# Small tiles padded to 64 bytes in a one-core decoder layer, and three small copies moved from VectorE to ScalarE

## The chip, the cores and the metric

One Trainium2 chip, one of its cores. The metric is device time in microseconds of one launch: the median of three runs of the kernel before is 544.61 us (544.2 to 545.45).

## What is computed

One layer of a decoder trunk over 256 tokens of width 1024, in float32. Cut to what matters here:

```
h = rms_norm(x, norm_mix_g)
u, q, kc, vc, ks, vs, kw, vw, gates, g_conv, g_attn = split(h @ w_in)
conv = silu(layer_norm(depthwise_conv31(u_a * sigmoid(u_g)))) @ conv_pw_w
k_cmp, v_cmp = compress(kc, ...), compress(vc, ...)      # 15 blocks of 32 tokens
    # compress: z = einsum(blocks + pos, w1); silu(z) @ w2
attn = gated sum of compressed, selected and window attention (16 heads, 4 groups)
x = x + (sigmoid(g_conv) * conv + sigmoid(g_attn) * attn) @ w_out
x = x + cross_attention(rms_norm(x), mem)                # 4 heads of 256
x = x + swiglu(rms_norm(x))                              # 1024 -> 2 x 2816 -> 1024
out = rms_norm(x)
```

## The kernel before

Nearly all of the time is matrix products with 1024 x 256 weight blocks. They run on TensorE in `float32r`, a type that goes through the array in one pass, and the accuracy of float32 is put together from three such products: each operand is split into a high part (ScalarE, a copy that rounds, L174 and L287) and a low part (the difference, VectorE L176 and L288, or GpSimd for a range of weights), and `hi*hi + hi*lo + lo*hi` is summed in PSUM. One `nc.tensor.matmul` has a stationary operand (`lhsT`, loaded into the array, shown as LDWEIGHTS, engine PEld) and a moving operand (`rhs`, streamed through it, shown as MATMUL, engine PE).

The stages in order of time: keys of the cross-attention (`ps_k`), the convolution's input (`ps_u`), the attention's projections (`ps_kc` to `ps_vw`), the gates mixed with the attention's scores and outputs (`ps_ga`, `ps_gc`, `ps_v`, and `s`, `pt`, `o`), the convolution's and the mixer's output projections (`ps_pw`, `ps_wo`), the cross-attention (`ps_xq`, `xs`, `xo_ps`, `ps_xo`), the feed-forward input (`ps_f`, L1200 with 512 moving columns and L1202 with 256), and its output (`fo`, `m`, L1239, mostly 512 columns). In all projections written as `rows` (L243) without `nat`, the weights are stationary and the activations moving; in `vs`, `vw` and `v0` to `v3` it is the other way round.

All tiles in SBUF come from one pool `sb`, through two helpers: `long` (activations and other tiles of 8 KB a partition, L121) and `small` (all others, L133). A tag names a place that tiles share one after the other. The pool lays the places out one behind the other in each partition, in the order in which the program first asks for them, and rounds each up to a multiple of 32 bytes. In the built program:

- `ppt`, `cpt`, `ones`, `eps_t` lie at bytes 1,152, 3,264, 4,032 and 4,544 of the partition. `eps_t` has two numbers and takes 32 bytes.
- So the fourteen places of the long tiles lie from 4,576 on, each at a multiple of 64 plus 32.
- `roots0`, one number at 127,456, takes 32 bytes as well. All larger places behind it begin at a multiple of 64 again: the high and low halves of weights from 127,488 on, the raw weights, the scores, the transposed probabilities.

Counted over the 3,819 matmul instructions of the built program, by the place in a 64-byte line at which the moving and the stationary operand begin:

| moving, stationary begin at (of 64) | instructions | which |
|---|---|---|
| 32, 0 | 2,834 | projections of L243 with stationary weights (2,064), L1200 (352), L1202 (352), cross scores `xs` (48), L607 (16), L331 (2) |
| 0, 32 | 631 | `vs`, `vw`, `v` of L243 (288), L1239 (207), L692 (32), L789 (24), L795 and L798 (64), L1080 (16) |
| 32, 32 | 201 | `xo_ps` of L967 (48), scores L732 and L734 (64), L1239 (48), L273 (16), L468 and L474 (9), L521 (16) |
| 0, 0 | 134 | transposes L777, L879 and L1004 (116), warm-up and small sums (18) |
| others | 19 | L521 (16, moving at 36), L709 (2), L341 (1) |

Of the 256-column `float32r` products, 2,480 are of the first kind, 335 of the second and 80 of the third; of the 512-column ones 352 (L1200), 183 (L1239) and 80 (L732 and L1239).

Three small copies touch the compression of keys and values. For `kc` and `vc` (the loop at L498) the four groups are copied from PSUM on ScalarE; a fifth column of the tile, `GROUPS`, is set to zero on VectorE (L505), and two entries of it are filled with the position code, a copy of 16 numbers a partition from `ppt` (L506). In `hidden` (L514), the values' hidden layer is written to `zz` four times over (L534), 240 numbers on 64 partitions. All three are `nc.vector.tensor_copy`. The scheduler of the framework places each instruction on its engine's queue by priority and by what it depends on, and an engine runs its queue in order. `convolve` (L441) puts the taps of the depthwise convolution behind everything else on VectorE, ScalarE and GpSimd, as filler; `behind` lets it start after the marks that it is given, one of which is the copy of L506.

Of the kernel before, what the change touches and what calls it, by code (L numbers as in the profile page):

```python
# [11 lines left out]
AF = mybir.ActivationFunctionType  # L12
# [3 lines left out]
P = 128  # L16
# [4 lines left out]
GROUPS = 4  # L21
HD = 64
# [7 lines left out]
BIG = 1e30  # L30
NCMP = 15
WARM = 8
FIRST_G = 18

CHUNKS = (
# [12 lines left out]
PP_POS = PP_DW + NB * TAPS  # L48
# [48 lines left out]
def tile_hybrid_block(  # L97
# [16 lines left out]
    nc = tc.nc  # L114
    PSUM = bass.MemoryType.PSUM
    sb = ctx.enter_context(tc.tile_pool(name="sb", bufs=1))
# [14 lines left out]
        return t, t[:, 0], t[:, 1]  # L131

    def small(name, shape, dt=F32, tag=None, bufs=1):  # L133
        return sb.tile(shape, dt, tag=tag or name, name=name, bufs=bufs)

    def bank(name):
# [8 lines left out]
    def aux(name, shape, tag, bufs):  # L145
        return axp.tile(shape, F32, tag=tag, name=name, bufs=bufs)

    def f(ap):
        return ap.bitcast(F32)


    ppt = small("ppt", [P, PP_END])
# [13 lines left out]
    def col(base, j):  # L166
        return ppt[:, base + j:base + j + 1]
# [15 lines left out]
    def behind(*marks):  # L183

        stack = ExitStack()
        for m in marks:
            stack.enter_context(tc.issue_after(m.ins))
        return stack
# [40 lines left out]
    def in_line():  # L229
        return behind(*last)  # L230
# [23 lines left out]
    def gemm(name, x, nat=False):  # L254

        ps = bank(f"ps_{name}")
        for i in range(2):
            sweep(ps, halved(name, i), x, i, nat, name in in_order)
        return ps
# [86 lines left out]
    warm = aux("warm", [P, P], "o", 1)  # L346
    for _ in range(WARM):
        nc.tensor.matmul(warm, lhsT=ones, rhs=ones, start=True, stop=True)
# [35 lines left out]
    for i in range(4):  # L384
        hs = slice(2 * i, 2 * i + 2)
        for kb in (2 * i, 2 * i + 1):
            vec = nc.vector.scalar_tensor_tensor(out=hf[:, kb], in0=xt_t[:, kb], scalar=col(PP_GMIX, kb),
                                                 in1=r1, op0=ALU.mult, op1=ALU.mult)
# [14 lines left out]
    zz = small("zz", [P, 2, 4 * 64], tag="pr", bufs=4)  # L403
# [33 lines left out]
    taps = range(TAPS)  # L437
    on_v = chain(taps_v(0, taps[FIRST_G:], part01), *[taps_v(j, taps, yt[:, j:j + 2]) for j in range(2, NB, 2)])
    on_g = taps_g(taps[:FIRST_G])

# [10 lines left out]
    for j in range(NB):  # L451
# [3 lines left out]
        vec = nc.vector.tensor_tensor(out=vt[j][:, PAD:], in0=ps[:, 0], in1=sg, op=ALU.mult)  # L455
# [42 lines left out]
    for kv, name in enumerate(("kc", "vc")):  # L498
        ps = gemm(name, h)
        kc = kvt[kv]  # L500
        for g in range(2):
            for odd in range(2):
                at = ps[HD * g:HD * g + HD].rearrange("p b (m l o) -> p b l m o", l=8, o=2)[:, :, :, :, odd]
                act = nc.scalar.activation(kc[HD * odd:HD * odd + HD, :, g:GROUPS:2].rearrange("p l b m -> p b l m"), at, AF.Copy)
        nc.vector.memset(kc[:, :, GROUPS], 0.0)  # L505
        vec = nc.vector.tensor_copy(kc[:, :, GROUPS, 0:2],  # L506
                                    ppt[:, PP_POS + 16 * kv:PP_POS + 16 * kv + 16].rearrange("p (m l) -> p l m", m=2))
        convolve(14, 1 - kv, act, vec)
    kcp = small("kcp", [P, GROUPS, 2, 16], F32R)
    vcs = small("vcs", [P, 2, 2, HD], F32R, tag="sg", bufs=3)  # L510
# [3 lines left out]
    def hidden():  # L514


        z_ps = aux("z_ps", [P, GROUPS + 1, NCMP], "o", 1)
        with in_line():
            for l in range(16):
                for kv in range(2):  # L520
                    mm = nc.tensor.matmul(z_ps[HD * kv:HD * kv + HD], lhsT=w1t[:, kv, l],  # L521
                                          rhs=kvt[kv][:, l % 8, :, l // 8:l // 8 + NCMP], start=l == 0, stop=l == 15)
        last[:] = [mm]
        zs = small("zs", [P, GROUPS, NCMP], tag="zs", bufs=2)
        at = small("at", [P, 1])
        nc.scalar.activation(at, z_ps[:, GROUPS, 0:1], AF.Copy)
        sig = nc.scalar.activation(zs, z_ps[:, :GROUPS], AF.Sigmoid, bias=at)

        with behind(sig):
            nc.scalar.activation(small("exps", [P, 1]), eps1, AF.Exp)  # L530
        z1 = zz[:HD, 0, :64].rearrange("p (g n) -> p g n", g=GROUPS)[:, :, 0:NCMP]
        nc.vector.scalar_tensor_tensor(out=z1, in0=z_ps[:HD, :GROUPS], scalar=at[:HD], in1=zs[:HD], op0=ALU.add, op1=ALU.mult)
        nc.vector.scalar_tensor_tensor(out=zs[HD:], in0=z_ps[HD:, :GROUPS], scalar=at[HD:], in1=zs[HD:], op0=ALU.add, op1=ALU.mult)
        nc.vector.tensor_copy(zz[HD:, 1].rearrange("p (g r n) -> p g r n", g=GROUPS, r=4)[:, :, :, 0:NCMP],  # L534
                              zs[HD:].unsqueeze(2).to_broadcast([HD, GROUPS, 4, NCMP]))

    def compressed():

# [15 lines left out]
    for j in range(4):  # L554
# [6 lines left out]
        vec = nc.vector.scalar_tensor_tensor(out=q1[0:64], in0=ps[64:128], scalar=-0.125, in1=f(q1[64:128]),  # L561
                                             op0=ALU.mult, op1=ALU.subtract)
# [269 lines left out]
    p = [scores(0)]  # L832
# [6 lines left out]
    vec = nc.vector.tensor_tensor(out=nsc, in0=nsc, in1=mc.unsqueeze(3).to_broadcast([P, 2, HEADS, 16]), op=ALU.subtract)  # L839
# [10 lines left out]
    vec = nc.vector.tensor_tensor(out=nsc, in0=nsc, in1=sumc.unsqueeze(3).to_broadcast([P, 2, HEADS, 16]), op=ALU.mult)  # L850
# [632 lines left out]
```

## Time and profile before

| | us |
|---|---|
| median of three runs | 544.61 |
| the profiled execution's own time | 544.99 |
| span of its trace | 542.9 |
| busy: TensorE (PE), weight loads (PEld) | 535.8, 502.0 |
| busy: VectorE, ScalarE, GpSimd | 455.8, 358.1, 155.5 |

An engine's row in the profile gives its busy time, its share of the span and its instructions. A matmul's record runs from its issue to the modelled end of its pipeline, so the records of a stream overlap; the pace of the stream is the distance between starts. The view that shows this best is the chain that ended last: a row of it holds a start, a length, and a count of matmuls that followed each other without a gap, so that length by count is the pace. The timeline shows starts and the records of each group, and behind them the idle time before it and what ended it.

### The profile page before, as it was taken

The page shows a single profiled execution, that of the slowest core. Times are in us where ns is not written, and L with a number is a line of the kernel's source. Part 1 is how long each engine was busy: PE and PEld are TensorE (multiplying, and loading weights), DVE is VectorE, ACT ScalarE, POOL GpSimd, SP SyncE. Part 2 cuts the span into 40 slices and gives each one's busy share as a digit, 9 for nine tenths or more (in the row PEclk, how much of TensorE's full clock was granted, in tenths as well). Part 3 has the DMA queues.
Part 4 walks back from the last instruction along what each step waited for, and adds up shares of the span by engine and source line. Part 5 has one row for each costly group of instructions (what it writes and reads, how often), then busy time and mean ns, then how long its engine had stood idle before and what let it go on. Part 6 is the DMA issues. An engine that isn't in the chain of part 4 may idle for free.

```text
span 542.9 us, 10515 instructions
## 1 busy us (share of the span) xinstructions
PE 535.8 (99%) x3963; PEld 502.0 (92%) x3963; DVE 455.8 (84%) x916; ACT 358.1 (66%) x646; POOL 155.5 (29%) x109
## 2 busy tenths in 40 slices
PE   9999999999999999999999999999999999999995
PEld 8999999999999998999999999988888888888884
DVE  4898999899889898975859676688899998879996
ACT  4676566678855977879447655566666677638563
POOL 0079999998990000300004000240000000000001
PEclk9999999999999999999999999999999999999999
DMA  8927955554424653347655642847756668438632
GB/s 317 403 86 243 366 170 180 201 184 156 154 99 150 203 173 112 123 137 214 222 190 165 240 155 89 233 145 219 246 168 202 195 209 234 146 122 235 195 121 78
DMA packets 30740, 101.52 MB, mean 187 GB/s; under 512 B 3297, under 2 KB 5857, under 8 KB 30305
## 3 DMA queue, kind: packets, MB, share of 16 engines
q1 hardware_dynamic: 29104, 96.99, 53.5%
q0 software_dynamic: 864, 2.62, 2.9%
q10 hardware_dynamic: 720, 1.23, 0.6%
q8 instruction: 31, 0.51, 0.4%
q14 instruction: 21, 0.16, 0.1%
HBM read 99.59 MB, written 1.25 MB: 186 GB/s over the span
## 4 chain that ended last, share of the span: by engine, by line
PE 61%; DVE 1%; ACT 0%; issue 0%; DVEq 0%; ACTq 0%
PE ps_f L1200 15%; PE ps_f L1202 8%; PE fo L1239 6%; PE ps_pw L243 4%; PE ps_xq L243 4%; PE ps_wo L243 4%; PE ps_xo L243 4%; PE ps_v L243 4%; PE m L1239 4%; PE xo_ps L967 1%; PE xs L967 1%; PE o L798 1%; PE pt_a L777 1%; PE s L732 1%; PE o L795 1%; PE pt_b L777 0%
## 5 line engine op out<-in xcount | busy, mean ns | idle before, releaser
L419 DVE SCALAR_TENSOR_TENSOR yp<-vt,ppt,yp 128x256 f32<-128x256 f32 x196 | 78.5, 483 | 0.3
L1200 PE MATMUL ps_f<-g,f_1h 128*128 128x512 f32 x176 | 49.0, 397 | 0.0
L1200 PE MATMUL ps_f<-g,f_0h 128*128 128x512 f32 x176 | 48.2, 395 | 0.0
L1200 PEld LDWEIGHTS ps_f<-g,f_1h 128*128 128x128 f32 x176 | 32.8, 188 | 7.6 <-ACT f_1h L174 0.2
L1200 PEld LDWEIGHTS ps_f<-g,f_0h 128*128 128x128 f32 x176 | 30.0, 188 | 4.0
L176 DVE TENSOR_TENSOR f_1l<-f,f_1h 128x1024 fp32r<-128x1024 f32 x22 | 27.4, 1248 | 5.9 <-ACT f_1h L174 4.9
L1202 PEld LDWEIGHTS ps_f<-g,f_0l 128*128 128x128 f32 x176 | 27.0, 189 | 3.9
L174 ACT ACTIVATE f_1h<-f 128x1024 fp32r<-128x1024 f32 x22 | 23.2, 1056 | 7.7 <-PE ps_xo L243 3.7
L1202 PE MATMUL ps_f<-g,f_0l 128*128 128x256 f32 x176 | 28.3, 282 | 0.0
L176 DVE TENSOR_TENSOR f_0l<-f,f_0h 128x1024 fp32r<-128x1024 f32 x22 | 26.8, 1219 | 1.7 <-ACT f_0h L174 1.7
L1202 PE MATMUL ps_f<-g,f_1l 128*128 128x256 f32 x176 | 26.5, 281 | 0.0
L176 POOL TENSOR_TENSOR u_0l<-u,u_0h 128x1024 fp32r<-128x1024 f32 x7 | 17.3, 2467 | 31.4 <-DVE kt L505 30.5
L1203 ACT ACTIVATE ab<-ps_f 128x256 f32<-128x256 f32 x44 | 16.5, 374 | 12.4 <-PE ps_f L1202 12.4
L174 ACT ACTIVATE f_0h<-f 128x1024 fp32r<-128x1024 f32 x22 | 23.1, 1050 | 1.5 <-PE ps_xo L243 1.3
L752 ACT ACTIVATE p<-p,mins 128x256 f32<-128x256 f32 x32 | 15.9, 504 | 12.1 <-DVE mins L737 12.1
L1202 PEld LDWEIGHTS ps_f<-g,f_1l 128*128 128x128 f32 x176 | 23.3, 188 | 0.0
L431 POOL TENSOR_TENSOR yt<-yt,vw 128x512 f32<-128x512 f32 x17 | 22.8, 1341 | 0.7 <-ACT vw L428 0.3
L1116 POOL DMA_DIRECT2D spare<-in_wfo_dram x1 | 0.9, 863 | 76.7 <-DVE ab L1204 76.7
L1204 DVE TENSOR_TENSOR ab<-ps_f,ab 128x256 f32<-128x256 f32 x44 | 18.2, 418 | 3.7 <-ACT ab L1203 3.4
L287 ACT ACTIVATE uh<-sl 128x256 fp32r<-128x256 f32 x22 | 9.1, 414 | 13.9 <-DVE sl L1208 13.8
L176 POOL TENSOR_TENSOR u_1l<-u,u_1h 128x1024 fp32r<-128x1024 f32 x7 | 17.9, 2554 | 0.0
L307 POOL TENSOR_TENSOR nt_l<-nr_l 128x2 f32<-128x2 f32 x4 | 1.0, 240 | 54.4 <-DVE nr_l L304 54.1
(658 smaller groups left out, 1709.4 us busy)
## 6 DMA issues: line engine op xcount, KB each, us to landing
f<-in_wst_dram SPq DMA_DIRECT2D x44, 512.0 KB, 5.5
fo<-in_wfo_dram SPq DMA_DIRECT2D x16, 512.0 KB, 3.9
u<-in_wst_dram SPq DMA_DIRECT2D x14, 512.0 KB, 8.1
q<-in_wst_dram SPq DMA_DIRECT2D x8, 512.0 KB, 5.5
ga<-in_wst_dram SPq DMA_DIRECT2D x8, 512.0 KB, 3.6
gc<-in_wst_dram SPq DMA_DIRECT2D x8, 512.0 KB, 3.8
v<-in_wst_dram SPq DMA_DIRECT2D x8, 512.0 KB, 6.6
pw<-in_wst_dram SPq DMA_DIRECT2D x8, 512.0 KB, 5.6
```

Source lines behind the costliest of these rows:

```text
L174: copy = nc.scalar.activation(hi, w, AF.Copy)
L176: splits[name] = copy, eng.tensor_tensor(out=lo, in0=w, in1=f(hi[:]), op=ALU.subtract)
L243: mm = nc.tensor.matmul(ps[:, b], lhsT=lhsT, rhs=rhs, start=row + b + kb == 0, stop=kb == NB - 1 and row == 2 and b == 1)
L419: nc.vector.scalar_tensor_tensor(out=out[:, i] if t == ts[-1] else acc[i], in0=v, scalar=w, in1=acc[i], op0=ALU.mult, op1=ALU.add)
L431: nc.gpsimd.tensor_tensor(out=yt[:, 0:2], in0=yt[:, 0:2], in1=pr, op=ALU.add)
L752: exp.append(nc.scalar.activation(p1[k][:, br], p1[k][:, br], AF.Exp, scale=-1.0, bias=mins[:, hd, 1, br:br + 1], accum_out=sums[:, hd, 1, ...
L967: mm = nc.tensor.matmul(o, lhsT=lhsT, rhs=rhs, start=n == 0, stop=n == len(order) - 1)
L1200: nc.tensor.matmul(ps, lhsT=hs[kb // 4][0][:, kb % 4, cs], rhs=fg[:, :, kb], start=kb == 0, stop=False)
L1202: nc.tensor.matmul(ps[:, 1], lhsT=hs[kb // 4][1][:, kb % 4, cs], rhs=fg[:, 0, kb], start=False, stop=kb == NB - 1)
L1203: nc.scalar.activation(ab[:, b], ps[:, 0], AF.Copy)
L1204: joins[b] = nc.vector.tensor_tensor(out=ab[:, b], in0=ps[:, 1], in1=ab[:, b], op=ALU.add)
L1239: mm = nc.tensor.matmul(o, lhsT=a[x], rhs=b[w], start=start and n == 0, stop=stop and n == 2)
```

## The change

`small` gives a tile of two dimensions with fewer than 16 numbers a partition a full 64 bytes, and returns the part that was asked for. The three copies become activations with the function Copy on ScalarE. Lines behind the first edit move down by one, behind the second by three.

```diff
+LINE = 16
...
     def small(name, shape, dt=F32, tag=None, bufs=1):
+        if len(shape) == 2 and shape[1] < LINE:
+            return sb.tile([P, LINE], dt, tag=tag or name, name=name, bufs=bufs)[:, 0:shape[1]]
         return sb.tile(shape, dt, tag=tag or name, name=name, bufs=bufs)
...
         nc.vector.memset(kc[:, :, GROUPS], 0.0)
-        vec = nc.vector.tensor_copy(kc[:, :, GROUPS, 0:2],
-                                    ppt[:, PP_POS + 16 * kv:PP_POS + 16 * kv + 16].rearrange("p (m l) -> p l m", m=2))
+        vec = nc.scalar.activation(kc[:, :, GROUPS, 0:2],
+                                   ppt[:, PP_POS + 16 * kv:PP_POS + 16 * kv + 16].rearrange("p (m l) -> p l m", m=2), AF.Copy)
         convolve(14, 1 - kv, act, vec)
...
-        nc.vector.tensor_copy(zz[HD:, 1].rearrange("p (g r n) -> p g r n", g=GROUPS, r=4)[:, :, :, 0:NCMP],
-                              zs[HD:].unsqueeze(2).to_broadcast([HD, GROUPS, 4, NCMP]))
+        nc.scalar.activation(zz[HD:, 1].rearrange("p (g r n) -> p g r n", g=GROUPS, r=4)[:, :, :, 0:NCMP],
+                             zs[HD:].unsqueeze(2).to_broadcast([HD, GROUPS, 4, NCMP]), AF.Copy)
```

In the built program of the change `eps_t` and `roots0` take 64 bytes each. The long tiles begin at 4,608, 32 bytes higher than before and each at a multiple of 64, and the weights begin at 127,552, 64 bytes higher and again at a multiple of 64. Of the 3,819 matmuls, 3,800 then have both operands at a multiple of 64; the other 19 begin inside a tile, at 4 or 40. No matmul, shape or type changes.

The order of instructions on TensorE, GpSimd and the DMA queue is the same as before. Only the three copies change their queue. On ScalarE, at the end of the cross-attention's keys and the start of the convolution's input (`u_0`, `u_1` are the halves of the weights of `u1` to `u3`, `kt` and `vt` the tiles of the copies; the brackets name the engines or DMA queues whose semaphores are waited for), the rows before are:

```order
L174 ACTIVATE u_0h<-u_0_498 128x1024 [waits DMAHW6_49,DVE_49,PE_49]
L287 ACTIVATE kxh<-ps_k_285 128x512 [waits PE_49]
L174 ACTIVATE u_1h<-u_1_528 128x1024 [waits DMAHW7_49,DVE_49,PE_49]
L174 ACTIVATE u_0h<-u_0_579 128x1024 [waits DMAHW0_49,DVE_49,PE_49]
L454 ACT_TABLE_LOAD
L454 ACTIVATE sg_413<-ps_u_356 128x256 [waits PE_49]
```

and with the change:

```order
L177 ACTIVATE u_0h<-u_0_498 128x1024 [waits DMAHW6_49,DVE_49,PE_49]
L290 ACTIVATE kxh<-ps_k_285 128x512 [waits PE_49]
L177 ACTIVATE u_1h<-u_1_528 128x1024 [waits DMAHW7_49,DVE_49,PE_49]
L509 ACTIVATE kt<-ppt 128x8x2 [waits DVE_49]
L509 ACTIVATE vt<-ppt 128x8x2 [waits DVE_49,Activation_49]
L177 ACTIVATE u_0h<-u_0_579 128x1024 [waits DMAHW0_49,PE_49]
L457 ACT_TABLE_LOAD
L457 ACTIVATE sg_413<-ps_u_356 128x256 [waits PE_49]
```

Both copies stand ahead of the split of the first half of `u3`, and wait for VectorE. On VectorE the same place before (`kxl` is the low part of the keys):

```order
L176 TENSOR_TENSOR u_1l<-u0w,u_1h 128x1024 [waits DMAHW3_49,Activation_49]
L506 COPY kt<-ppt 128x8x2 [waits DVE_49]
L288 TENSOR_TENSOR kxl<-ps_k_285,kxh 128x512 [waits Activation_49]
L505 MEMSET vt 128x8x16 [waits DVE_49]
L506 COPY vt<-ppt 128x8x2 [waits DVE_49]
L455 TENSOR_TENSOR vt_344<-ps_u_356,sg_413 128x256 [waits Activation_49]
```

loses the two COPY rows and is otherwise unchanged; the memset of `vt`, for which the second copy now waits on ScalarE, stays there. In `hidden`, the third copy leaves VectorE's queue (there it stood between two taps of the convolution) and stands on ScalarE behind `exps`, ahead of the split of the second half of `ks`, waiting for VectorE's `zs`.

## The prediction

> **What bounds the kernel now.** I read the profile's page first: busy times, the slices, and the shares of the chain that ended last.
>
> ```profile
> PE 535.8 (99%) x3963; PEld 502.0 (92%) x3963; DVE 455.8 (84%) x916; ACT 358.1 (66%) x646; POOL 155.5 (29%) x109
> ...
> PEclk9999999999999999999999999999999999999999
> ...
> PE 61%; DVE 1%; ACT 0%; issue 0%; DVEq 0%; ACTq 0%
> ```
>
> TensorE streams matmuls for 535.8 of 542.9 us at full granted clock, and the chain is made of TensorE's rows; the other engines have 1% of it. What an engine other than TensorE saves is worth nothing unless TensorE waits for it somewhere, and it waits almost nowhere. So the time is the number of matmuls, which stays, by their pace. The change can move the time only through the pace, that is through the place at which operands begin, or by making TensorE wait. I therefore read the pace in the chain of waits in order of time, where each row has a length and a count of matmuls without a gap, and compare rows whose operands begin differently in their 64-byte lines.
>
> ```profile
> 213.19 2.83 PE ps_v L243 x24
> 217.73 2.81 PE ps_v L243 x24
> 221.94 2.83 PE ps_v L243 x24
> 226.52 2.80 PE ps_v L243 x24
> ...
> 238.53 4.68 PE ps_v L243 x40
> ...
> 272.77 17.04 PE ps_wo L243 x144
> ...
> 304.49 1.42 PE xs L967 x12
> ...
> 316.30 1.43 PE xo_ps L967 x12
> ...
> 325.26 1.43 PE xo_ps L967 x12
> ...
> 328.11 1.42 PE xs L967 x12
> ...
> 340.37 14.20 PE ps_xo L243 x120
> ...
> 481.12 1.86 PE ps_f L1200 x8
> 482.98 0.95 PE ps_f L1202 x8
> ...
> 527.43 6.76 PE fo L1239 x29
> ```
>
> With 256 moving columns: `ps_wo`, `ps_xo` and `xs` (moving operand at 32, stationary at 0) go at 17.04 / 144, 14.20 / 120 and 1.42 / 12, all 118.3 ns each, and L1202 at 0.95 / 8 = 118.8. The `ps_v` rows (moving at 0, stationary at 32) make 15.95 us for 136, or 117.3. `xo_ps` (both at 32) goes at 1.43 / 12 = 119.2. With 512 columns, L1200 (moving at 32, stationary at 0) goes at 232.5, `fo` (moving at 0, stationary at 32) at 6.76 / 29 = 233.1. No row has both at 0 with this type and this many columns, so the state that the change makes isn't in the trace. One row of the same chain has both at 0, the transposes of the cross-attention, with 128 columns:
>
> ```profile
> 321.99 0.44 PE xpt L1004 x4
> ```
>
> 0.44 / 4 = 110 ns is what a load of 128 stationary columns allows where the moving operand takes less time than it.
>
> **The pace of matmuls with 256 columns.** There are 2,480 with the moving operand at 32 and the stationary one at 0. Between `xo_ps` (32, 32) and `ps_v` (0, 32) only the moving operand's start differs, and 119.2 - 117.3 = 1.9 ns is its price. Between `xo_ps` and `xs` (32, 0) only the stationary operand's start differs, and 119.2 - 118.3 = 0.9 ns is its price. If both prices are real and add up, both at 0 goes at 118.3 - 1.9 = 116.4 ns. The stationary operand's price is uncertain: the scores are (32, 32) too, and in the timeline of TensorE four of them go from 155.00 to 155.46, 115 ns each.
>
> ```profile
> 154.54 0.39 PE L732 MATMUL s<-kdh,qt 128*128 128x512 f32 x1
> 154.77 0.40 PE L732 MATMUL s<-kdl,qt 128*128 128x512 f32 x1
> 155.00 0.28 PE L734 MATMUL s<-kdh,qt 128*128 128x256 f32 x1
> ...
> 155.46 1.10 PE L243 MATMUL ps_ga<-hh,ga_0h 128*128 128x256 f32 x8
> ```
>
> If the stationary start costs nothing, the moving start is the whole difference of `ps_v` to `ps_wo`, and both at 0 goes at 117.3. I take the middle of 116.4 and 117.3, 116.8, so 1.5 ns less than 118.3: 2,480 x 1.5 ns = 3.7 us. The 335 products with (0, 32) can gain from the stationary operand alone, 0 to 0.9 ns, 0.15 us in the middle. The 80 with (32, 32) gain 119.2 - 116.8 by the `xo_ps` rows and nothing by the scores', 0.1 us. Ends of the three together: 2,480 x 1.0 = 2.5 us and 2,480 x 1.9 + 335 x 0.9 + 80 x 2.8 = 5.2 us.
>
> **The pace with 512 columns.** There are 615. Here the moving operand at 0 isn't faster: 233.1 against 232.5, the other way by 0.6, and the scores (32, 32) take 155.00 - 154.54 = 0.46 us for two, 230 each. I take zero, with 0.6 x 615 = 0.4 us as the bound on either side.
>
> **The three copies.** In VectorE's timeline they are:
>
> ```profile
> 34.76 2.37 DVE L506 COPY kt<-ppt 128x16 f32<-128x16 f32 x1
> 37.05 0.68 DVE L288 TENSOR_TENSOR kxl<-ps_k,kxh 128x512 fp32r<-128x512 f32 x1
> 37.70 0.17 DVE L505 MEMSET vt<- 128x128 f32 x1
> 37.90 1.59 DVE L506 COPY vt<-ppt 128x16 f32<-128x16 f32 x1
> ...
> 105.39 0.29 DVE L533 SCALAR_TENSOR_TENSOR zs<-z_ps,at,zs 64x60 f32<-64x60 f32 x1
> ...
> 106.62 2.33 DVE L534 COPY zz<-zs 64x240 f32<-64x240 f32 x1
> ```
>
> VectorE loses 2.37 + 1.59 + 2.33 = 6.3 us of busy time. On the path this is worth nothing: no wait of TensorE in the chain is for VectorE there. ScalarE gets three copies. Their price there isn't in the trace; the nearest rows are L527 below, 60 numbers in 0.31 us, and the taps and `qt` copies of up to 0.6 us, so I take 0.3 each, and 0.6 as the bound. ScalarE's timeline around the two places:
>
> ```profile
> 33.13 1.06 ACT L174 ACTIVATE u_1h<-u 128x1024 fp32r<-128x1024 f32 x1
> 37.57 1.06 ACT L174 ACTIVATE u_0h<-u 128x1024 fp32r<-128x1024 f32 x1 [3.38 <-DMA u<-in_wst_dram]
> ...
> 103.34 0.31 ACT L527 ACTIVATE zs<-z_ps,at 128x60 f32<-128x60 f32 x1
> 103.67 1.28 ACT L530 ACT_TABLE_LOAD   x1
> 104.96 0.20 ACT L530 ACTIVATE exps<-eps_t 128x1 f32<-128x1 f32 x1
> 105.27 1.06 ACT L174 ACTIVATE ks_1h<-ks 128x1024 fp32r<-128x1024 f32 x1
> 108.11 1.06 ACT L174 ACTIVATE kw_0h<-kw 128x1024 fp32r<-128x1024 f32 x1 [1.78 <-PE ps_q L243]
> ```
>
> The first two stand between the splits at 33.13 and 37.57, where ScalarE sits idle for 3.38 us until a transfer lands. The second waits for VectorE's memset of `vt`. That memset ended at 37.87, but with the 2.37 us copy gone from ahead of it VectorE reaches it at 35.4 and ends it near 35.6; ScalarE is free again by 36.2 at most, before the transfer at 37.57. Behind the waiting copy are the split of `u3`, the table load and the sigmoid of `u0`; none moves. If that cover were gone, the split would start as late as the memset, which is 0.3 us after 37.57. The third copy waits for `zs`, ready at 105.39 + 0.29 = 105.68, so ScalarE waits 0.5 us, copies, and starts `ks_1h` near 106.1 instead of 105.27. The idle 1.78 us ahead of `kw_0h` takes that up, and TensorE first reads `ks_1h` here:
>
> ```profile
> 117.33 1.11 PE L243 MATMUL ps_ks<-hh,ks_1h 128*128 128x256 f32 x8
> ```
>
> That is 10 us later. The copies cost nothing, with 0.3 us as the upper bound. As for what is late next: over two stretches, by windows (time, then busy time of PE, PEld, DVE, ACT and POOL):
>
> ```profile
> 100.00:146.00 46.00, 46.00 (x437) 45.78 (x435) 45.45 (x102) 36.13 (x59) 43.25 (x24) 1.00 0.51 169
> ...
> 354.00:476.00 122.00, 122.00 (x701) 106.43 (x701) 109.56 (x191) 81.75 (x144) 6.26 (x6) 1.00 0.62 196
> ```
>
> VectorE is busy for 45.45 of 46 us in the first, minus the copy's 2.33 = 43.1; TensorE gaining 1.3% makes the stretch 45.4, so VectorE still fits. In the second it has 12 us to spare.
>
> **Sum.** 3.7 + 0.15 + 0.1 + 0 + 0 = 3.95 us off the profiled execution, whose own time is 544.99 (span 542.9 and 2.1 around it): 541.0. It lies 0.4 above the median of the runs, 544.61, so I forecast 544.61 - 3.95 = 540.6 us.
>
> **Rival 1: nothing moves.** The differences between the rows come from which tiles meet, not from the 32 bytes; then (0, 0) goes like (32, 0), at 118.3 and 232.5, and the time is 544.6, within 1 us. For it: the 512-column rows show no gain at all, and the scores with both at 32 go at 115. Against it: `ps_wo`, `ps_xo` and `xs` at three places agree at 118.3, and all five `ps_v` rows are faster. [...] The `ps_v` rows, 1.0 ns faster, speak a little against it, and I keep it at 0.24.
>
> **Rival 2: a much larger gain.** One misplaced operand of the two may be enough to slow the stream, so that the three states in the trace are all slow and (0, 0) is another regime. The pace would fall toward what the load allows, 110 ns in the `xpt` row: 2,480 x 8.3 ns = 20.6 us, and 615 x (232.5 - 2 x 110) = 7.7 us, 28 us in all and 516 us, which I call an estimate from that row. Before it got there VectorE would bind in the windows above (109.56 of 122), so half of it, some 530 us, is likelier than all. [...] Against it: with the moving operand at 0, `fo` should have shown part of that, and it is the slowest. I give it 0.18. [...]
>
> **Rival 3: slower.** `xs` and `xo_ps` can be read the other way: in `xo_ps` moving and stationary operand begin at the same place of a line, and go at 119.2; in `xs` and in `ps_v` they begin half a line apart, and go at 118.3 and 117.3. If the same phase is what costs, the change puts all 3,800 matmuls into it: 2,480 x 0.9 + 335 x 1.9 = 2.9 us, 547.5 us. It decides from 0.44 ns a matmul on (0.2% of 544.61 is 1.09 us, by 2,480). Against it: the scores, in the same phase, at 115. I give it 0.13.
>
> That the change doesn't place operands as it says is no rival: the built program's addresses show it.
>
> **How the numbers follow.** The forecast, a gain of 2 to 6 us, has 0.45, the rivals 0.24, 0.18 and 0.13. A measurement of this kernel tells about 0.2%, so 543.5 to 545.7 is no change. Faster: nearly all of the forecast, all of rival 2 and a little of rival 1, 0.63. Same: most of rival 1 and the edge of the forecast, 0.24. Slower: rival 3, 0.13. The range holds the forecast (538.6 to 542.6, wider by the bounds of 512 columns and copies), rival 1, and the near half of rival 2 to 530; at the top it ends at 546, which leaves out rival 3 and the far part of rival 2, a little under 0.2 together. The likeliest case's own range is 538 to 543.
>
> **What would show it.** In the profile after: the 24-matmul rows of L243 at 2.80 us (116.8 each) instead of 2.84, the same for `xs`, `xo_ps`, L1202 and `ps_v`, and L1200 still at 1.86 for 8. The three copies on ScalarE under 0.6 us each, the splits of `u3` and `ks` in time, and TensorE without new waits. I am wrong if those rows stay at 118.3, if L1200 falls below 1.84, or if the gain sits in a wait that ended.

## The result, and the profile after the change

The median after the change is 542.31 us over 11 runs (538.59 to 545.96), beside 544.90 us for the kernel before over 11 runs (544.2 to 545.97). The ratio is 0.9943 with a 95% interval of 0.9916 to 0.9969. The runs of the kernel before lie within 1.8 us, those of the changed kernel within 7.4 us: three at 538.59 to 539.81 with a mean granted clock of 0.997 to 0.999, seven at 541.87 to 542.99 and one at 545.96, these eight with 0.988 to 0.995. The profiled execution is one of the seven, with an own time of 542.99 us and a span of 540.7.

The profile's page of the changed kernel: busy times, and the granted clock in 40 slices of the span.

```profile
PE 529.8 (98%) x3963; PEld 495.4 (92%) x3963; DVE 455.0 (84%) x913; ACT 357.6 (66%) x649; POOL 155.7 (29%) x109
...
PEclk9999999999979999999999999999999999999999
```

TensorE is busy for 6.0 us less, and one slice of the clock, the twelfth (149 to 162 us), has a 7 that wasn't there. So two things have happened: a pace and a wait.

**The pace.** The chain of waits in order of time, with the groups that the prediction read (start, length, group, count):

```profile
215.60 2.73 PE ps_v L246 x24
220.04 2.83 PE ps_v L246 x24
...
273.98 16.32 PE ps_wo L246 x144
...
304.86 1.41 PE xs L970 x12
...
316.67 1.44 PE xo_ps L970 x12
...
340.44 14.13 PE ps_xo L246 x120
...
375.79 1.86 PE ps_f L1203 x8
377.65 1.36 PE ps_f L1205 x12
...
525.44 6.67 PE fo L1242 x29
```

`ps_wo` goes at 16.32 / 144 = 113.3 ns, where it had 118.3, and L1205 at 113.3. But `ps_xo`, with operands placed in the same way, goes at 117.8. `ps_v` has both: 113.8 in one row, 117.9 in the next. So the stream now has two regular paces, about 113.3 and about 117.8 ns. It holds one of them until it is interrupted, and starts again in one or the other. L1203 with 512 columns stays at 232.5, `fo` falls from 233.1 to 230.0.

The next table puts all `float32r` products with 256 columns together. It is worked out from the starts of all records in a trace (a `float32r` product leaves one, 2,352 for the 2,352 of L243 before; those of L273, in `float32`, leave two each, 32 for 16, 216 ns apart): the mean distance from one start to the next, distances over 135 ns (waits, other shapes) left out. "Distance" is the place of the moving operand minus that of the stationary one, within 128 bytes; the prediction counted within 64.

| kernel | moving, stationary begin at (of 128) | distance | products | mean pace |
|---|---|---|---|---|
| before | 96, 0 | 96 | 2,480 | 118.40 ns |
| before | 0, 96 | 32 | 335 | 117.05 |
| before | 96, 96 | 0 | 80 | 118.30 |
| after | 0, 64 | 64 | 2,480 | 114.86 |
| after | 64, 0 | 64 | 335 | 116.76 |
| after | 0, 0 | 0 | 80 | 118.68 |

In the 2,480, about 1,620 distances after the change are 113 or 114 ns and some 780 are 117 to 119. The gain is 2,480 x 3.54 ns = 8.8 us. The 80 are of two kinds, which their mean hides: `xo_ps` goes at 119.2 before and 119.8 after, the scores, in groups of four, at 116.9 in both.

**The copies.** ScalarE's timeline at the first two places, and at the third:

```profile
34.10 0.21 ACT L509 ACTIVATE kt<-ppt 128x16 f32<-128x16 f32 x1
35.69 0.22 ACT L509 ACTIVATE vt<-ppt 128x16 f32<-128x16 f32 x1 [1.39 <-DVE vt L508]
37.66 1.06 ACT L177 ACTIVATE u_0h<-u 128x1024 fp32r<-128x1024 f32 x1 [1.75 <-DMA u<-in_wst_dram]
...
106.09 0.41 ACT L537 ACTIVATE zz<-zs 64x240 f32<-64x240 f32 x1 [1.25 <-DVE zs L536]
```

They take 0.21, 0.22 and 0.41 us where VectorE took 2.37, 1.59 and 2.33. The split of `u3` starts when its transfer lands, as forecast.

**The wait.** TensorE waited for next to nothing in the middle of the kernel before. Now the view of its waits has two new rows (group, who releases it: us, times, longest), and the windows show the stretch around them (time, busy of PE, PEld, DVE, ACT and POOL, then the granted clock); first after, then before:

```profile
PE s L735 <- DVE nsc L698: 2.0, 1, 2.0
PE s L737 <- ACT sgt L715: 1.8, 1, 1.8
```

```profile
146.00:158.00 12.00, 8.21 (x53) 7.08 (x53) 11.97 (x25) 5.64 (x10) 8.98 (x6) 0.80 0.52 184
```

```profile
146.00:158.00 12.00, 12.00 (x103) 11.83 (x101) 8.57 (x16) 6.11 (x11) 11.45 (x8) 1.00 0.33 109
```

TensorE stands still for 3.8 of 12 us, and its granted clock is 0.80 in the stretch. The trace's record of the clock shows what that mean hides: 1.00 until 153.09 us, then 0.50 for 6.83 us, until 159.92. TensorE waits for 1.79 us of these; the other 5.0 at half clock, where products with 256 columns start 213 or 214 ns apart, cost another 2.5. Compared matmul by matmul, the changed kernel is 3.2 us ahead at 100 us, 3.6 ahead at 149.5, and 2.95 behind at 161: 6.5 us are lost. To see where it comes from, follow the releasers backward through the timelines of VectorE, ScalarE and GpSimd:

```profile
138.30 8.05 DVE L179 TENSOR_TENSOR ga_0l<-ga,ga_0h 128x1024 fp32r<-128x1024 f32 x1
146.28 5.18 DVE L422 SCALAR_TENSOR_TENSOR yp<-vt,ppt,yp 128x256 f32<-128x256 f32 x13
...
152.15 0.87 DVE L698 TENSOR_TENSOR nsc<-cs_ps,nsc 128x256 f32<-128x256 f32 x2
```

```profile
150.45 1.06 ACT L177 ACTIVATE ga_0h<-ga 128x1024 fp32r<-128x1024 f32 x1 [6.27 <-DMA ga<-in_wst_dram]
...
155.86 0.24 ACT L715 ACTIVATE sgt<-gt_ps 128x96 f32<-128x96 f32 x1
```

```profile
137.20 2.46 POOL L179 TENSOR_TENSOR ga_0l<-ga,ga_0h 128x1024 fp32r<-128x1024 f32 x1
139.56 2.11 POOL L679 TENSOR_TENSOR vcm<-vcs,cpt 128x512 fp32r<-128x512 f32 x2
141.57 2.46 POOL L179 TENSOR_TENSOR ga_1l<-ga,ga_1h 128x1024 fp32r<-128x1024 f32 x1
143.92 6.31 POOL L434 TENSOR_TENSOR yt<-yt,vw 128x512 f32<-128x512 f32 x4
```

One split on VectorE, the low part of `ga2`'s first half, takes 8.05 us. In the kernel before the same instruction took 1.71:

```profile
139.98 1.71 DVE L176 TENSOR_TENSOR ga_0l<-ga,ga_0h 128x1024 fp32r<-128x1024 f32 x1
```

GpSimd runs beside it without a pause until 145.27, where the first of the additions to `yt` is over and the next starts 0.08 us later. The split ends 1.08 us behind 145.27, and the addition that runs beside its end takes 2.14 us, where the one before took 1.35. Behind the split VectorE's queue is late, so `nsc`, which TensorE's first scores wait for, comes at 152.15. The split also frees the place of the raw weights late: the transfer that goes into it is issued at 146.38, and the copy for which ScalarE then waits 6.27 us stands ahead of `sgt`, the second thing that TensorE waits for. The 8.05 us agree with a split that was blocked while GpSimd ran, and not for one of GpSimd's instructions alone: the split ends at 146.35, behind the first of the four additions to `yt`, so five of GpSimd's instructions had gone before it.

**The balance** of the profiled executions, summed over the distances from one matmul's start to the next: 8.6 us are gained outside the stretch from 149.5 to 161 us, 8.3 of them by the 2,480 products and 0.5 by L1242, less some smaller losses; 6.5 are lost in the stretch. (The 8.8 above leave breaks in the stream out; the 8.3 have them in, 0.35 us at 299.4 us among them.) That leaves 2.05 us, where the spans differ by 2.2. Of the 6.5, the two waits make 3.8 and the half clock 2.5.

### The profile page after: what moved, and what is told of

Its sections match the earlier page's. It is cut to its first block, busy times and chain, and to the rows that moved or that the text cites. A ratio compares the mean times of both kernels' runs of the same rounds, so it can differ in the third digit from the quotient of the medians.

```text
span 540.7 us, 10518 instructions
## 1 busy us (share of the span) xinstructions
PE 529.8 (98%) x3963; PEld 495.4 (92%) x3963; DVE 455.0 (84%) x913; ACT 357.6 (66%) x649; POOL 155.7 (29%) x109
## 4 chain that ended last, share of the span: by engine, by line
PE 60%; DVE 1%; ACT 0%; issue 0%; ACTq 0%; DVEq 0%
PE ps_f L1203 15%; PE ps_f L1205 7%; PE fo L1242 6%; PE ps_xo L246 4%; PE ps_v L246 4%; PE ps_pw L246 4%; PE ps_wo L246 4%; PE ps_xq L246 4%; PE m L1242 4%; PE xo_ps L970 1%; PE xs L970 1%; PE o L801 1%; PE pt_a L780 1%; PE s L735 1%; PE o L798 1%; PE pt_b L780 0%
## 5 line engine op out<-in xcount | busy, mean ns | idle before, releaser
L1203 PE MATMUL ps_f<-g,f_1h 128*128 128x512 f32 x176 | 49.0, 397 | 0.0
L1203 PE MATMUL ps_f<-g,f_0h 128*128 128x512 f32 x176 | 48.3, 396 | 0.0
L1203 PEld LDWEIGHTS ps_f<-g,f_1h 128*128 128x128 f32 x176 | 32.9, 188 | 7.6
L1203 PEld LDWEIGHTS ps_f<-g,f_0h 128*128 128x128 f32 x176 | 29.9, 188 | 4.0
L1205 PEld LDWEIGHTS ps_f<-g,f_0l 128*128 128x128 f32 x176 | 26.8, 188 | 3.9
L1205 PE MATMUL ps_f<-g,f_0l 128*128 128x256 f32 x176 | 27.4, 277 | 0.0
L434 POOL TENSOR_TENSOR yt<-yt,vw 128x512 f32<-128x512 f32 x17 | 25.2, 1482 | 3.0 <-ACT vw L431 2.7
L1205 PE MATMUL ps_f<-g,f_1l 128*128 128x256 f32 x176 | 25.8, 277 | 0.0
L755 ACT ACTIVATE p<-p,mins 128x256 f32<-128x256 f32 x32 | 15.9, 503 | 10.3 <-DVE mins L740 10.3
L1205 PEld LDWEIGHTS ps_f<-g,f_1l 128*128 128x128 f32 x176 | 22.6, 188 | 0.0
```

Of the source, the lines that this page charges most:

```text
L434: nc.gpsimd.tensor_tensor(out=yt[:, 0:2], in0=yt[:, 0:2], in1=pr, op=ALU.add)
L755: exp.append(nc.scalar.activation(p1[k][:, br], p1[k][:, br], AF.Exp, scale=-1.0, bias=mins[:, hd, 1, br:br + 1], accum_out=sums[:, hd, 1, ...
L1203: nc.tensor.matmul(ps, lhsT=hs[kb // 4][0][:, kb % 4, cs], rhs=fg[:, :, kb], start=kb == 0, stop=False)
L1205: nc.tensor.matmul(ps[:, 1], lhsT=hs[kb // 4][1][:, kb % 4, cs], rhs=fg[:, 0, kb], start=False, stop=kb == NB - 1)
```

## Experiments

### The two halves of the change, each alone

The copies without the padding:

```diff
     def small(name, shape, dt=F32, tag=None, bufs=1):
-        if len(shape) == 2 and shape[1] < LINE:
-            return sb.tile([P, LINE], dt, tag=tag or name, name=name, bufs=bufs)[:, 0:shape[1]]
```

> The three copies on ScalarE, no padding. Theory (the padding does it all): all paces as before, 118.3 ns with 256 columns, and the time of before within 0.2% (544 to 545.5), unless VectorE running ahead by 2 us wakes the wait near 150 us, then up to 4 us slower. Rival (the copies matter): 1 us or more faster than before.

Measured: 544.98 us over 11 runs, ratio 0.9998 (0.9989 to 1.0006), span 542.7. In the layout of before the copies are worth nothing, as the prediction said.

The padding without the copies:

```diff
-        vec = nc.scalar.activation(kc[:, :, GROUPS, 0:2],
-                                   ppt[...], AF.Copy)
+        vec = nc.vector.tensor_copy(kc[:, :, GROUPS, 0:2], ppt[...])
...
-        nc.scalar.activation(zz[HD:, 1]..., zs[HD:]..., AF.Copy)
+        nc.vector.tensor_copy(zz[HD:, 1]..., zs[HD:]...)
```

> The padding alone, all three copies back on VectorE. Theory (the padding does it all): the same paces as with the whole change, 113.3 or 117.8 ns a matmul of 256 columns, and a time 2 to 5 us under the kernel before, within 1.5 us of the whole change. Rival (the copies matter): at least 2 us slower than the whole change. The wait at the first scores, near 150 us, depends on a race between VectorE and GpSimd and may come or not; without it the time is near 538.

Measured: six runs, two at 538.43 and 539.12 us and four at 550.94 to 556.43; the profile was of the best, without a wait. The median, 552.6 us, is 10.3 above that of the changed kernel, so the copies matter, as the rival had it, but a loss against the kernel before was in neither theory. To find its cause, the same kernel was profiled once more:

> The same kernel as in the first run with the padding alone (the three copies back on VectorE), one more look, because its six runs fell into two heaps, 538.4 and 539.1 us on one side, 550.9 to 556.4 on the other. Theory S (a wait): while GpSimd works without a pause, a split of VectorE (two inputs in SBUF) can be kept out for several of GpSimd's instructions; TensorE then waits for VectorE, and its granted clock falls for a while. By it an execution above 550 us shows at least one split of VectorE of 5 us or more between 100 and 160 us, and waits of TensorE of more than 8 us in sum there, with the pace of the 256-column products at 115 to 116 ns as in the good execution. Rival P (a lottery of paces): the slow executions are those whose streams fall into the slower of the two paces, without new waits; by it a slow one shows 118 ns nearly throughout. P alone can't come above the 545 us of the kernel before, which goes at 118.4 throughout. If this look falls at 538 to 540 us, it tells nothing new.

Measured: 556.18 us, span 554.1. VectorE's timeline holds the third copy, the view of TensorE's waits what came of it:

```profile
107.01 19.79 DVE L537 COPY zz<-zs 64x240 f32<-64x240 f32 x1
```

```profile
PE ps_vs L246 <- DVE qt L564: 8.1, 1, 8.1
PE s L737 <- ACT sgt L715: 2.3, 1, 2.3
PE ps_ga L246 <- POOL ga_0l L179: 1.7, 1, 1.7
...
PE ps_ga L246 <- POOL ga_1l L179: 1.0, 1, 1.0
```

The copy of 240 numbers takes 19.79 us and ends at 126.80. GpSimd ran ten instructions back to back from 106.43 on, and this row of its timeline is the last of them, over at 126.66:

```profile
124.32 2.34 POOL L179 TENSOR_TENSOR vw_1l<-vw,vw_1h 128x1024 fp32r<-128x1024 f32 x1
```

In the kernel before, the same copy was let in at 108.81, when the split of `ks`'s second half was over and GpSimd had to wait for ScalarE:

```profile
109.25 2.40 POOL L176 TENSOR_TENSOR kw_0l<-kw,kw_0h 128x1024 fp32r<-128x1024 f32 x1 [0.44 <-ACT kw_0h L174]
```

The copy ended at 108.95, inside that pause of 0.44 us. In the slow execution `kw_0l` follows without a pause, and so do eight more. Theory S holds (it is a copy that was kept out, not a split). The 256-column products have 114.87 ns here, the same as in the changed kernel, so the lottery of paces is not the reason. The copies are worth nothing before, but with a faster TensorE, on VectorE, five of seven executions are 11.8 us or more slower than the other two. Only one of the five was profiled; that the other four have the same cause is not shown.

### What place of the operands makes the pace

Only `eps_t` padded, so that the activations begin at 0 and the weights at 32 of 128 (`if name == "eps_t":` in place of the condition in `small`, copies as before):

> Only eps_t takes 64 bytes, so that the long tiles begin at a multiple of 64 and all behind roots0 at 32: most matmuls have the moving operand at 0 and the stationary one at 32. Copies on ScalarE. Theory A (both operands have to be at a multiple of 64 for the fast pace): 116.6 to 117.5 ns with 256 columns as in the ps_v rows of before, no stretch at 113.3, and 1.5 to 4 us under before. Theory B (the moving operand alone decides): stretches at 113.3 as with the whole change, 5 us or more under before where no wait comes.

Measured: 544.70 us over 11 runs, ratio 0.9996 (0.9988 to 1.0005); the 2,480 at 118.40 ns.

```profile
273.19 17.04 PE ps_wo L246 x144
```

A moving operand at a multiple of 64 is worth nothing by itself. The distance is 0 - 32 = 96 of 128, what it was before, and so is the pace, to a hundredth.

Only `roots0` padded, so that activations begin at 96 and weights at 32 (`if name == "roots0":`):

> Only roots0 takes 64 bytes, so that nearly all matmuls have both operands at 32. Copies on ScalarE. Theory A (both at a multiple of 64): no stretch at 113.3, paces of 117 to 119.5 ns with 256 columns, and a time within 2 us of before. Theory C (the two operands have to begin at the same place of a line): stretches at 113.3 as with the whole change.

Measured: 542.76 us over 6 runs, ratio 0.9945 (0.9926 to 0.9965); the 2,480 at 114.92 ns, in the two regular paces, and the same two waits near 150 us (2.07 and 1.67 us).

```profile
274.14 16.32 PE ps_wo L246 x144
...
340.67 14.13 PE ps_xo L246 x120
```

No operand of the weights' products begins at a multiple of 64 here, and the whole effect is there. So the multiple of 64 isn't what counts; the two operands' places relative to each other are. At this point two readings were left: the same place within 64 bytes, or a distance of 64 within 128.

The tile of the first root at 128 bytes, so that both begin at 0 of 128:

```diff
-        return nc.scalar.activation(small(name, [P, 1]), eps_t[:, 0:1], AF.Sqrt)
+        return nc.scalar.activation(sb.tile([P, 2 * LINE], F32, tag=name, name=name)[:, 0:1], eps_t[:, 0:1], AF.Sqrt)
```

> The changed kernel with the first tile for a root at 128 bytes instead of 64, so that the weights begin at a multiple of 128 like the activations; in the changed kernel they begin 64 behind one. Theory L (only the place within 64 bytes counts): the same time and paces as the changed kernel, 538.5 to 543 us, ratio 0.992 to 0.997, 256-column mean 115 to 116 ns. Rival M (the place within 128 bytes counts): in the profile of the changed kernel the products whose two operands both begin at a multiple of 128, xo_ps, go at 120 ns, and those with 64 between them at 113 to 118; by M nearly all of the 2,863 go at 120 here, 1.6 ns above the 118.4 of the kernel before, and the time is 547 to 550 us.

Measured: 546.83 us over 6 runs, ratio 1.0033 (1.0022 to 1.0045). Slower than before, with 3,800 matmuls at a multiple of 64 as in the change, and 64 bytes of padding more. From the chain:

```profile
275.13 17.09 PE ps_wo L246 x144
...
306.94 1.43 PE xs L970 x12
...
342.90 14.24 PE ps_xo L246 x120
```

`ps_wo` goes at 118.7, and all 2,895 products with 256 columns have 118.96 in the mean, spread from 115 to 122 like those of before. Theory L falls, and M holds in its direction; its size (120) was that of one group.

The streams by themselves. The kernel computes nothing of the layer.

```diff
+ for m in (0, 8, 16, 24):            # start of the moving operand, in numbers of 4 bytes
+     for s in (0, 8, 16, 24):        # start of the stationary operand
+         x, w = mov[:, m:m + 1024], sta[:, s:s + 1024]
+         48 matmuls into one bank; ScalarE reads it; the next stream waits for that
```

> Nothing of the layer is computed: the kernel is 80 streams of 48 products with 256 columns, each with a load of 128 columns, from two tiles, with the moving and the stationary operand beginning at 0, 32, 64 or 96 bytes past a multiple of 128, all 16 pairs, five times over; between two streams TensorE waits for ScalarE to read PSUM. Theory L: the eight pairs at the same place of a 64-byte line run in one of two regular paces, 113.3 or 117.8 ns, constant within a stream and different from stream to stream; the eight others at about 118.3 ns in all five. Rival M: the four pairs that are alike within 128 bytes go at 120, the four that differ by 64 at 113 to 118, the rest at 118.3. Rival R (it is not the addresses but the kernel's two tiles' roles): no pair differs from another by more than 1 ns.

Measured: the second of five repeats in the chain. The names give the two starts in bytes; all 48 products are alike, and a start or end of a stream takes the same in each.

```profile
115.72 5.98 PE m0s0r L41 x48
122.43 6.04 PE m0s32r L41 x48
129.20 5.73 PE m0s64r L41 x48
135.66 5.88 PE m0s96r L41 x48
...
155.70 6.03 PE m32s64r L41 x48
162.47 5.93 PE m32s96r L41 x48
169.13 5.74 PE m64s0r L41 x48
175.61 5.97 PE m64s32r L41 x48
182.31 5.97 PE m64s64r L41 x48
...
202.48 5.74 PE m96s32r L41 x48
```

Over the five repeats, streams with a distance of 64 take 5.72 to 5.74 or 5.93 us, the others 5.88 to 6.04 (but for the very first, partly at half clock). At a distance of 96 the streams take 6.03 or 6.04 us in all but one pair, and over 48 products 6.04 - 5.73 is 6.5 ns each, where the layer has 118.4 - 113.3 = 5.1. At a distance of 0 they take 5.97 or 5.98 in 18 of 20, a little less than at 96; in the layer 0 is the slower of the two. (64, 0) and (96, 32) took the short time in all five repeats, (0, 64) in two, (32, 96) in none. So the fast pace needs no tile of the layer and no work of the other engines beside it. Rival R falls, and so does theory L, as no stream at a distance of 0 is fast. That the fast pace goes with a moving operand in the upper half was tried next.

`eps_t` at 128 bytes: activations at 64, weights at 0.

```diff
-    eps_t = small("eps_t", [P, 2])
+    eps_t = sb.tile([P, 2 * LINE], F32, tag="eps_t", name="eps_t")[:, 0:2]
```

> The changed kernel with the tile of eps_t at 128 bytes, so that the activations begin at 64 of a 128-byte line and the weights at 0; in the changed kernel it is the other way round. Theory D (the distance of the two starts within 128 bytes sets which paces there are; 64 gives the two regular ones): the 256-column products stay at 114.5 to 116 ns in the mean, partly fast and partly slow, and the time stays between 538 and 546 us with the waits near 150 us. Rival U (the moving operand in the upper half always gives the fast pace): in the streams by themselves the pairs (64, 0) and (96, 32) were fast in all ten cases, (0, 64) and (32, 96) in two of ten; by U the 2,480 products with stationary weights go at 113.5 throughout, 1.4 ns or 3.4 us less than in the changed kernel, 535 to 539 us where no new wait comes, and GpSimd, full already, then makes TensorE wait between 60 and 150 us.

Measured: 542.93 us over 10 runs (539.51 to 544.77), ratio 0.9973 (0.9961 to 0.9985); the 2,480 at 115.71 ns, half of them slow. U falls: in the layer a moving operand in the upper half doesn't always give the fast pace. What chooses one of the two paces at the start of a stream stays open. The profile, of the run with 539.51 us, shows no wait near 150 us and the split at 1.71 us, span 537.3: that is the changed kernel's case of 538.6 to 539.8 us.

### The wait at 150 us

`ga2`'s low parts on GpSimd, `aside` up to `"ga3"` instead of `"ga2"`:

> The changed kernel with the low parts of one more weight block, ga2, on GpSimd instead of VectorE; that is the split that took 8.05 us on VectorE in the profile of the changed kernel. On TensorE nothing moves. Theory S: TensorE no longer waits behind VectorE near 150 us; the time falls to that of the best executions of the changed kernel, 537.5 to 539.5 us with a spread under 2 us, ratio 0.987 to 0.990, clock 0.997 or more. Rival P: the spread and the 542 us come from the lottery of paces and stay, ratio 0.993 to 0.996. Rival G: GpSimd, which is full there, becomes late with ga2's low parts (2.4 us each instead of 1.2), and TensorE waits for GpSimd instead, 542 us or more.

Measured: 545.50 us over 12 runs, ratio 1.0010 (0.9996 to 1.0024). The split that was kept out is gone, and the next one takes its place, that of `ga3`:

```profile
145.41 6.45 DVE L179 TENSOR_TENSOR ga_0l<-ga,ga_0h 128x1024 fp32r<-128x1024 f32 x1 [1.11 <-ACT ga_0h L177]
```

```profile
PE s L737 <- ACT sgt L715: 4.8, 1, 4.8
```

My expectation from theory S failed: more work on GpSimd lengthened the stretch without a pause. The wait that came is again for VectorE's blocked split, by way of the transfer and ScalarE, whose copy of `gc` waits 6.94 us for it, not for GpSimd itself.

Less work on GpSimd, `FIRST_G = 8` instead of 18, alone and together with `eps_t` at 128 bytes:

> The changed kernel with 8 of the convolution's first taps on GpSimd instead of 18; VectorE takes the other ten for two blocks, 20 instructions of about 0.48 us, and ScalarE loses 20 of 0.45. Theory S (VectorE's split is kept out while GpSimd runs without a pause): from 100 us on GpSimd has five additions of 1.3 us less until 144 us and six less behind, so that it pauses; no split of VectorE takes more than 3 us between 100 and 160 us, TensorE doesn't wait near 150 us, and the time is 537 to 539.5 us with a spread under 2 us, ratio 0.986 to 0.990. Rival V (VectorE, 44.6 of 46 us busy from 100 to 146 us, becomes the bound with 9.6 us more): TensorE waits for VectorE at 150 to 200 us, 542 us or more. Rival N: the pauses of GpSimd are too short, the split is still kept out in most executions, 541 to 543 us as in the changed kernel.

> Both edits of the two other kernels of this call: activations at 64 and weights at 0 of a 128-byte line, and 8 taps on GpSimd. By U and S together 534 to 536 us, ratio 0.980 to 0.984. By D and S the same as with fewer taps on GpSimd alone, 537 to 539.5 us. By V or N not under 540 us.

Measured: 544.94 us over 12 runs, ratio 1.0004 (0.9994 to 1.0015), and for both edits 545.59 us over 10 runs, ratio 1.0012 (1.0000 to 1.0025). The split takes 2.24 us in the first and 2.56 in the second, and TensorE doesn't wait at 150 us, as S had it, but V decides the time. In the first, VectorE's timeline and TensorE's:

```profile
136.62 2.24 DVE L179 TENSOR_TENSOR ga_0l<-ga,ga_0h 128x1024 fp32r<-128x1024 f32 x1
```

```profile
184.80 2.06 PE L780 MATMUL pt_a<-cpt,p 128*128 128x128 f32 x8 [4.79 <-DVE p L769]
```

The last kernel gives VectorE four taps instead of ten, and moves GpSimd's other four behind the gates' splits:

```diff
-FIRST_G = 18
+FIRST_G = 14
...
-        convolve(11, (1, 0, 1, 1)[j], act, vec)
+        convolve(11, 0, act, vec)
...
-        convolve(11, 1 - br, act, vec)
+        convolve(11, 0, act, vec)
```

> The changed kernel with four of GpSimd's eighteen taps given to VectorE (eight instructions of about 0.48 us) and the four that stood between 100 and 134 us put behind the gates' splits, to 144 us; ScalarE's and TensorE's order from 136 us on is as in the changed kernel. With ten taps given to VectorE TensorE waited 4.79 us for VectorE at 185 us, but VectorE's split at 136 us was not kept out (2.24 us). Theory S: GpSimd pauses between 100 and 135 us, VectorE's split of ga2 takes under 3 us, TensorE doesn't wait at 150 us; VectorE has 3.8 us more to do, less than the 4.8 us by which 9.6 us more were too much, so that no wait comes at 185 us either: 537 to 539.5 us, spread under 2 us, ratio 0.986 to 0.990. Rival V: VectorE is late all the same, a wait of 1 us or more at 170 to 190 us, 540 to 543 us. Rival N: the split is kept out as before, 541 to 543 us with waits at 150 us.

Measured: 537.18 us over 4 runs (536.74 to 539.07), ratio 0.9850 (0.9834 to 0.9866). That is faster than both kernels. VectorE's split, and all of TensorE's waits in the profile:

```profile
138.50 1.81 DVE L179 TENSOR_TENSOR ga_0l<-ga,ga_0h 128x1024 fp32r<-128x1024 f32 x1
```

```profile
PE warm L351 <- DVE eps_t L160: 1.1, 1, 1.1
PE ps_f L1203 <- ACT f_1h L177: 0.3, 1, 0.3
PE pt_b L780 <- DVE mins L745: 0.2, 1, 0.2
```

The 2,480 go at 115.70 ns here, 0.84 slower than in the profile of the changed kernel, and the span is 537.0 against 540.7 all the same. So the wait, not the lottery of paces, is what separates 542 from 538 us. The other profiles agree: the padded kernels profiled at 538.43 and 539.51 us had no wait near 150 us, those at 542.99 and 543.28 had one.

The time is the one that theory S gave, but its reason is not what the profile shows. GpSimd pauses five times for 0.4 us or more between 103 and 128 us, and not at all between 128 us and the split at 138.50. The split came 0.72 us before the end of GpSimd's running instruction and was let in there, without a pause, as in the kernel before. Why it came at such a moment in all four runs, if it did, is not known.

## Why the prediction was right, and where its steps failed

The time came out where it was forecast, 542.3 in a range of 530 to 546 and on the faster side, but 540.6 was the sum of wrong terms: 8.6 us of gain where it had 3.95, and a loss of 6.5 us that it didn't have. That the two errors nearly cancelled is luck.

- **The pace with 256 columns, 1.5 ns each.** Measured 3.5. The step that failed is the reading of the rows: "only the moving operand's start differs, and 119.2 - 117.3 = 1.9 ns is its price." By these prices the moving operand at 0 and the stationary one at 32 of 64 would go at 117.3, and both at 32 at 119.2; the 2,480 went at 118.40 and at 114.92 there. What differed between `xo_ps`, `ps_v` and `xs` was the distance of the two operands within 128 bytes (0, 32 and 96), and no row of the kernel before had 64. The prices of two starts can't be added, because neither has one: where the distance is the same, other starts gave the same pace (118.40 in two kernels with 96, 114.86 and 114.92 in two with 64). The scores, which had made the prediction doubt, go at 116.9 over all 32 of their 256-column products, where the four in its lines had 115; why products at the same distance, 0, differ by 2 to 3 ns is open.
- **"So the state that the change makes isn't in the trace."** Right, and rival 2 was right that the missing state could be another regime: 113.3 ns is one. Its size was wrong. The 110 ns that the prediction took for the load (in the kernel before, loads of 128 columns start 111 ns apart in the median where 32 columns move, in `cs_ps`, and 109 where 128 do, in `pt_a` and `pt_b`) were not reached, and a third of the products stayed at the slower of the two paces.
- **Rival 3, the same phase costs.** It was set aside, and it is what the chip does when the distance is 0: 118.96 ns and 546.83 us, where it had named 547.5. It did not come because the weights stand 64 behind within 128 bytes, and at that distance the 2,480 went at 114.86 ns. The change gains by an accident of its sizes: 64 bytes more in one small tile turn 542.3 into 546.8.
- **512 columns, zero.** L1203 stayed at 232.5 (232.47 to 232.75 in the mean). The 183 products of L1242 gained 2.8 ns, 0.5 us, a little over the bound of 0.4.
- **The 335 and the 80.** The 335 gained 0.3 ns, the 80 nothing. Together 0.1 us, where 0.25 was forecast.
- **The copies, nothing.** Right for the layout of before (0.9998). With the faster TensorE it fails, and the row that told it was quoted: 2.33 us for 240 numbers, which ScalarE does in 0.41. Nearly six times as long as another engine needs was the mark of an instruction kept waiting inside its own record: GpSimd's split of `ks`'s second half ended at 108.81, the copy at 108.95.
- **"VectorE is busy for 45.45 of 46 us ... so VectorE still fits."** This step failed and cost 6.5 us. It took VectorE's busy time for work. The same window had GpSimd at 43.25 of 46 us; the question to ask was who of the two waits for the other when TensorE brings their work closer together. VectorE's busy time fell by 0.8 us instead of 6.3, since the 8.05 us of the blocked split, 6.3 more than before, count as busy.

That the blocking is the cause of the wait is shown by all the profiles together: in the four with a VectorE instruction of over 6 us TensorE waits behind it, and in the nine where the split takes 2.56 us or less it doesn't wait near 150 us, those with fewer taps on GpSimd among them. What the two engines share there, no run shows.

## What to carry to other kernels

Where many products run back to back, look at where both operands begin relative to each other, not at either alone (118.40 ns at a distance of 96 here, 114.86 at 64), and measure the distances before padding: a layout found by accident can be lost by the next tile, as here, where 64 bytes more in one small tile turn 542.3 us into 546.8. When a change makes the bounding engine faster, look for pairs of engines that are both near full beside it (45.45 and 43.25 of 46 us here), and ask whether an instruction that is too long for its size was kept waiting (8.05 us, where the same split took 1.71). Work that is worth nothing to move off such an engine can become worth 10 us in the median (552.6 against 542.3) once the bounding engine is faster.

## What the runs showed of the hardware that was not expected

- The pace of the 2,480 `float32r` products with 256 columns went with the distance of the two operands within 128 bytes: 118.98 ns at 0, 118.40 at 96, and at 64 one of two regular paces, 113.3 or 117.8 ns, that held until the stream was interrupted. In the layer a distance of 32 was seen only with the operands' roles swapped, at 117.05. Whether the period is 128 bytes or longer wasn't tried.
- A VectorE instruction was kept out over several of GpSimd's: 19.79 us behind ten of them, 8.05 us behind five. In all four blocks of over 6 us it was let in at the first moment at which no record of GpSimd ran: a pause of 0.08 us in three, the end of its work in the fourth. In all thirteen profiles of the layer the split ended 1.08 or 1.09 us after the end of the instruction of GpSimd at which it was let in. In seven profiled executions VectorE's split came 0.4 to 0.7 us before the end of GpSimd's running instruction, and was let in at that end; in six the blocked instruction came 1.15 to 1.85 us before, and was let in at that end only in the two with eight taps on GpSimd. What decides whether it gets in without a pause wasn't tried.
- The granted clock of TensorE fell beside its longer waits, and stayed low for longer than they lasted: in each of the six profiles of the layer with a wait of 2.0 us or more it was 0.50 for 6.83 us (10.24 at the wait of 8.1 us), and in the seven without such a wait it stayed at 1.00 between the first 8 and the last 7 us.
